# Gates and output projection of a hybrid decoder block rewritten as seven-block products in fp16 parts

## The chip, the cores and the metric

The kernel runs on one core of a Trainium2 chip. Its metric is the device time of one execution in microseconds, from three runs; beside it stands one execution taken by the hardware profiler. The engines are TensorE (matmuls; PE in rows), VectorE (DVE), ScalarE (ACT), GpSimd (POOL) and SyncE (SP, which issues the transfers). Each works through its own instructions in a fixed order.

## The reference, cut to what matters

One layer, 2048 positions of 1024 channels, float32:

```python
h = rmsnorm(x, norm_mix_g)
(lru_x, lru_gate, m_qk, m_v, m_o, m_i, m_f,
 s_q, s_k, s_v, g_a, g_b, g_c) = split(h @ w_in)          # g_*: 1024 columns each
ya = (rg_lru(conv(lru_x)) * gelu(lru_gate)) @ w_out_lru       # 256 -> 1024
yb = (sigmoid(m_o) * mlstm(conv(m_qk), m_v, ...)) @ w_out_mlstm
yc = stick_breaking_attention(s_q, s_k, s_v) @ w_out_sb
merged = sigmoid(g_a) * ya + sigmoid(g_b) * yb + sigmoid(g_c) * yc
x = x + merged @ w_o
hf = rmsnorm(x, norm_ffn_g)
gate, up = split(hf @ w_ffn_in)                            # 2 x 2816 columns
x = x + (silu(gate) * up) @ w_ffn_out
out = rmsnorm(x, final_norm_g)
```

## The kernel before

Channels lie on the 128 partitions, positions on the free axis, in four chunks of 512 (`CH`). Three stages follow one another.

**S** goes chunk by chunk: projections of h (`psd`), the mLSTM (`m`), the linear recurrence (`L`, `l`), attention of the chunk before (`a`, `attn`), the norm of the next chunk (`t`), and queries, keys and values (`S`); `ORD` is that order. Attention works in pieces of one head and one chunk of keys: per piece four score tiles (`pz`, two matmuls each), two sigmoids on ScalarE (`ka`, `be`), a scan on VectorE (`cb`), the product `be` x `cb` in turn on VectorE and GpSimd, transposes on TensorE (`pt`), a split into two parts (`ah` on ScalarE, `al` on VectorE) and eight matmuls into `pav`. Attention of the last chunk stands behind S in the code.

**G** and **G_out** go chunk by chunk too. Operands are float32 split into a high and a low part of type float32r; `dense` (L189) issues three matmuls per term, high by high, high by low, low by high. `weights` (L168, L176) loads each weight tile again for each chunk and splits it. A gate tile (`pg`, 24 matmuls) goes through a sigmoid and is multiplied by its branch projection (`py`, 6 matmuls); `po` is the output projection.

**F**, the feed-forward part, works on pairs of chunks. Two 2 x 2 block matrices are multiplied with seven block products instead of eight (`STEPS`, `blocks`), each product three fp16 matmuls per term (`product`, L864 to L866). `wforms` loads four weight blocks, forms their sums on GpSimd (`sm`), finds a power-of-two scale (a sum of squares, a one-column matmul `pse`, small integer steps `sce`, `scx`, `scf`) and writes seven blocks in two fp16 parts (`wh` on ScalarE, `wl` on VectorE). `F_input` does the same for the activations (`xq`, `tt`, `f`). F1 writes its results in such parts to DRAM (`fs` to `dA`); F2 reads them (`f<-dA`) once the scales of all of them are known.

A tile framework keeps dependences and buffers and sets each engine's order from the order of the code. PSUM has eight buffers of 128 x 512: two `d`, one `m`, two `z`, two `s`, one `av`. In G, `py` uses `m` for the first two chunks and `z` for the others, `pg` uses `d`.

## Time and profile before

| what | us |
|---|---|
| median of 3 runs (3026.48 to 3029.7) | 3026.51 |
| the profiled execution | 3026.73 |
| its span, first to last instruction | 3025.0 |
| TensorE busy in the span | 2838.8 |
| VectorE busy | 1962.6 |
| ScalarE busy | 1318.9 |
| GpSimd busy | 728.1 |

The span is shorter than the execution's time by 1.7 us. An engine is busy while an instruction with work runs on it; time in which it waits for a buffer or an input is not counted. The mean granted clock of TensorE was 0.963 of full speed.

### The profile page before, as it was taken

To read this page: it belongs to the slowest core of one execution; us is meant where nothing else is said; L and a number is where in the kernel's file an instruction comes from. 1 tells how busy PE (TensorE), PEld (TensorE's weight loads), DVE (VectorE), ACT (ScalarE), POOL (GpSimd) and SP (SyncE) were. 2 spreads that over 40 slices of the span, in tenths; PEclk is the share of its full clock that TensorE was granted. 3 is DMA by queue.
4 is the path that set the end of the run, shared out by engine and by line. 5 is a ranking of instruction groups with operands and counts; after the bars stand their busy time and mean duration, and the time that the engine had idled before them with its cause. 6 is when DMAs were issued, how large, how long until landed. Compare 5 with 4: busy or idle time off the path is not lost.

```text
span 3025.0 us, 36457 instructions
## 1 busy us (share of the span) xinstructions
PE 2838.8 (94%) x13405; PEld 1870.1 (62%) x13405; DVE 1962.6 (65%) x2793; ACT 1318.9 (44%) x1975; POOL 728.1 (24%) x876
## 2 busy tenths in 40 slices
PE   8999999999999999999998479999999996899996
PEld 7777878777877887888887134444444442344443
DVE  7677888987777765345343875555555554657667
ACT  4445464644554543223222444444444452434432
POOL 0022323322232210000000653233233231323221
PEclk9999999999999999999999699999999998899998
DMA  5454545354355325335324211222222226336433
GB/s 174 149 175 144 185 139 166 118 168 169 108 169 171 105 91 188 115 97 194 100 94 169 78 66 66 77 77 84 77 84 85 79 77 250 143 146 257 181 116 143
DMA packets 153171, 398.85 MB, mean 132 GB/s; under 512 B 18176, under 2 KB 38656, under 8 KB 144800
## 3 DMA queue, kind: packets, MB, share of 16 engines
q1 hardware_dynamic: 152992, 396.53, 38.0%
q8 instruction: 105, 1.72, 0.2%
q14 instruction: 74, 0.61, 0.1%
HBM read 307.79 MB, written 88.67 MB: 131 GB/s over the span
## 4 chain that ended last, share of the span: by engine, by line
PE 81%; DVE 8%; DMA 5%; issue 3%; ACT 2%; POOL 1%; SPq 0%; DVEq 0%; ACTq 0%; POOLq 0%
PE pfp L864 7%; PE pfp L866 7%; PE pfp L865 7%; PE pg L197 6%; PE pg L195 6%; PE pg L196 6%; PE pfq L864 3%; PE pfq L866 3%; PE pfq L865 3%; PE psd L195 3%; PE psd L197 3%; PE psd L196 3%; PE pt L689 2%; PE pfr L864 2%; PE pfr L865 2%
## 5 line engine op out<-in xcount | busy, mean ns | idle before, releaser
L176 DVE TENSOR_TENSOR wl<-wraw,wh 128x768 fp32r<-128x768 f32 (+2 forms) x232 | 285.1, 1230 | 282.7 <-ACT wh L168 281.9
L168 ACT ACTIVATE wh<-wraw 128x768 fp32r<-128x768 f32 (+2 forms) x232 | 238.6, 1030 | 462.0 <-PE pg L196 202.3
L864 PE MATMUL pfp<-f,wh 128*128 128x512 f16 x1056 | 403.4, 383 | 35.7 <-ACT f L908 22.4
L865 PE MATMUL pfp<-f,wh 128*128 128x512 f16 x1056 | 404.1, 383 | 8.3 <-DVE f L909 8.3
L866 PE MATMUL pfp<-f,wl 128*128 128x512 f16 x1056 | 401.0, 383 | 0.0
L864 PEld LDWEIGHTS <-wh 128*128 128x128 f16 x1848 | 182.3, 99 | 266.4 <-issue 34.3
L866 PEld LDWEIGHTS <-wl 128*128 128x128 f16 x1848 | 181.8, 98 | 235.7 <-issue 15.7
L865 PEld LDWEIGHTS <-wh 128*128 128x128 f16 x1848 | 182.1, 99 | 231.6 <-issue 24.1
L197 PE MATMUL pg<-hh,wl 128*128 128x512 f32 x768 | 305.5, 398 | 2.8 <-DVE wl L176 2.8
L195 PE MATMUL pg<-hh,wh 128*128 128x512 f32 x768 | 305.8, 399 | 1.2 <-ACT sgg L725 0.7
L196 PE MATMUL pg<-hl,wh 128*128 128x512 f32 x768 | 303.1, 395 | 1.6 <-POOL hl L176 1.6
L864 PE MATMUL pfq<-f,wh 128*128 128x512 f16 x528 | 201.7, 382 | 13.2 <-ACT wh L811 9.4
L866 PE MATMUL pfq<-f,wl 128*128 128x512 f16 x528 | 200.9, 382 | 4.1 <-DVE wl L812 4.1
L865 PE MATMUL pfq<-f,wh 128*128 128x512 f16 x528 | 201.9, 382 | 0.6 <-DVE f L909 0.6
L195 PE MATMUL psd<-hh,wh 128*128 128x512 f32 x448 | 183.9, 411 | 2.8 <-DVE scl L315 2.8
L826 POOL TENSOR_TENSOR sm<-raw 128x512 f32<-128x512 f32 (+1 forms) x46 | 66.1, 1436 | 496.8 <-DVE wl L812 380.1
L197 PE MATMUL psd<-hh,wl 128*128 128x512 f32 x448 | 180.8, 403 | 0.5 <-DVE wl L176 0.5
L196 PE MATMUL psd<-hl,wh 128*128 128x512 f32 x448 | 180.0, 402 | 0.0
L811 ACT ACTIVATE wh<-raw,scf 128x512 f16<-128x512 f32 (+1 forms) x154 | 116.1, 771 | 126.1 <-PE pfp L865 52.4
L197 PEld LDWEIGHTS pg<-hh,wl 128*128 128x128 f32 x768 | 145.8, 190 | 39.2 <-DVE wl L176 5.2
L196 PEld LDWEIGHTS pg<-hl,wh 128*128 128x128 f32 x768 | 144.7, 188 | 35.8 <-POOL hl L176 2.0
L195 PEld LDWEIGHTS pg<-hh,wh 128*128 128x128 f32 x768 | 144.6, 188 | 33.2 <-ACT sgg L725 0.9
(301 smaller groups left out, 6105.2 us busy)
## 6 DMA issues: line engine op xcount, KB each, us to landing
wraw<-in_wG SPq DMA_DIRECT2D x96, 512.0 KB, 3.5
f<-dA SPq DMA_DIRECT2D x22, 1792.0 KB, 14.5
wraw<-in_wS SPq DMA_DIRECT2D x56, 512.0 KB, 3.6
x<-in_xT SPq DMA_DIRECT2D x88, 256.0 KB, 4.0
raw<-in_wF SPq DMA_DIRECT2D x22, 1024.0 KB, 4.8
dA<-fs SPq DMA_DIRECT2D x44, 512.0 KB, 2.6
dA<-fs SPq DMA_DIRECT2D x22, 768.0 KB, 3.4
wraw<-in_wO SPq DMA_DIRECT2D x32, 512.0 KB, 5.3
```

Source lines behind the costliest of these rows:

```text
L168: nc.scalar.activation(dst, src, AF.Copy)
L176: (self.nc.gpsimd if pool else self.nc.vector).tensor_tensor(lo, src, hi.bitcast(F32), op=ALU.subtract)
L195: nc.tensor.matmul(ps, wh, hh, start=start and i == 0, stop=False)
L196: nc.tensor.matmul(ps, wh, hl, start=False, stop=False)
L197: nc.tensor.matmul(ps, wl, hh, start=False, stop=stop and i == n - 1)
L689: PE.transpose(pt[:, i * P : (i + 1) * P], As[i][:, js], self.idn)
L811: self.nc.scalar.activation(hi, x, AF.Copy, scale=s)
L826: G.tensor_tensor(sm[:, 0], a21, a22, op=ALU.add)
L864: mm(ps, wh[:, i, ks], f[:, j, 0], start=start and k == 0, stop=False, skip_group_check=True)
L865: mm(ps, wh[:, i, ks], f[:, j, 1], start=False, stop=False, skip_group_check=True)
L866: mm(ps, wl[:, i, ks], f[:, j, 0], start=False, stop=k == n - 1, skip_group_check=True)
```

## The change

Gates, branch projections and output projection are done like F: on pairs of chunks, seven block products, three fp16 matmuls per term. In the two pairs `gates` goes through 12 weight items (channel quarter i by branch), each 7 blocks of 12 matmuls and, four times 6 matmuls, the branch projection of the item before (`mix`, tile `py`). `project` has 6 items. `wforms` becomes a generator: `advance` steps it between block products, two items ahead, and steps other queues of work (`fill`) at a set rate: the attention of chunks 2 and 3 (0.45) beside the gates of the first pair, the inputs of the next product (0.9, 1.3), the parts of F1's results (0.8). Branch outputs y are stored once in float32 (`put_y`), and `y_parts` splits them per pair. The merged quad goes to DRAM in fp16 parts (`dM`) and is loaded as `mf`. The gates' inputs of the first pair, `H(0)`, are formed behind S. Scales of F2 and of the projection are per group (`scales`). In phase "G", `s` of PSUM has one buffer, for attention's `pt`; `pfq` takes the other (`q`), and `py`, `pse` and `pfr` take `m`.

```diff
+OSTEPS = [(0, 0, 3), (1, 0, 3), (0, 3, 1), (1, 3, 1), (2, 0, 4), (3, 0, 4)]
...
-    ORD = ["mLlatS"] * 4
+    ORD = ["mLltS", "mLlatS", "mLlatS", "mLlS"]
     PT = 6
-    NP = dict(d=2, m=1, z=2, s=2, av=1)
-    GT = "mzds"
+    NP = dict(d=2, m=1, z=2, s=1, q=1, av=1)
...
+    def psum(self, tag, name):
+
+        if tag == "s" and self.phase != "G":
+            tag = "sq"[self.flip]
+            self.flip ^= 1
+        return self.ps.tile([P, CH], F32, tag=tag, name=name, bufs=self.NP[tag])
...
-    def put_y(self, pool, i, c, y):
-        th = pool.tile([P, CH], FR, tag="yh", name="yh", bufs=1)
-        tl = pool.tile([P, CH], FR, tag="yl", name="yl", bufs=1)
-        self.split(th, tl, y, "A")
-        cs = slice(c * CH, (c + 1) * CH)
-        self.nc.sync.dma_start(self.dY[i, 0, :, cs], th.bitcast(F32))
-        self.nc.sync.dma_start(self.dY[i, 1, :, cs], tl.bitcast(F32))
+    def put_y(self, i, c, y):
+        self.nc.sync.dma_start(self.dY[i, :, c * CH : (c + 1) * CH], y)
...
                         As.append(at)
+                    yield
                     for j in range(NB):
...
+    def wforms(self, src, n, off, more=None):
...
+        yield
+        if more and self.gx:
+            mraw = more_load()
+        acc = self.cp.tile([P, 1], BF, tag="wacc", name="wacc", bufs=2)
...
+        yield
+        f = self.power(self.exponent(acc), off() if callable(off) else off)
+        m = f.shape[-1] - 1
+        w = ((wh, wl), f[:, m : m + 1])
+        yield
         if m == 1:
...
+    def next_weights(self):
+        k = self.at
+        w = self.work.pop(k).finish()
+        self.at = k + 1
+        self.load_item(k + 2)
+        if k + 1 in self.work:
+            self.work[k + 1].step()
+        return w
+
...
+    def advance(self):
+        if self.at in self.work:
+            self.work[self.at].step()
+        for f in list(self.fills):
+            f[2] += f[1]
+            while f[2] >= 1.0:
+                f[2] -= 1.0
+                f[0].step()
+            if f[0].done:
+                self.fills.remove(f)
...
+    PSG = dict(p="d", q="q", r="m")
...
+    def seven(self, q, t, put):
+
+        G = self.nc.gpsimd
+        b12, b11, b21, b22 = [q[:, i] for i in range(4)]
+        G.tensor_tensor(t, b12, b11, op=ALU.subtract)
+        put(B11, b11)
+        yield
+        put(T1, t)
+        G.tensor_tensor(t, b22, t, op=ALU.subtract)
+        yield
...
+            for (u, j), at in self.PLACE.items():
+                x = q[:, at]
+                V.scalar_tensor_tensor(x, x, gs[:, k + 4 * j : k + 4 * j + 1], R[u], op0=ALU.mult, op1=ALU.mult)
+            q0, kk = q, k
+            k = kk + 1
+            if k < KT // 2:
+                q = load()
+            yield
+            f = slot()
+            out.append(f)
+            yield from self.seven(q0, tt(), lambda i, x: self.split2(f[:, i, 0], f[:, i, 1], x))
+
...
+            for u in (1, 0):
+                y = self.gx.tile([P, 2, 2, CH], F16, tag="yt", name="ys", bufs=3)
+                self.split2(y[:, :, 0], y[:, :, 1], q[:, 2 * u : 2 * u + 2], s)
+                nc.sync.dma_start(self.dYs[cp, br, u], y)
...
+        def mix(n, br, ys, wm, inv, sg, aq):
+            u, j = [(1, 0), (1, 1), (0, 0), (0, 1)][n]
+            ps = self.psum("m", "py")
+            for k in range(2):
+                c = slice(k * 256 + j * P, k * 256 + j * P + P)
+                y = ys[u]
+                mm = nc.tensor.matmul
+                mm(ps, wm[:, 0, c], y[:, k, 0], start=k == 0, stop=False)
+                mm(ps, wm[:, 0, c], y[:, k, 1], start=False, stop=False)
+                mm(ps, wm[:, 1, c], y[:, k, 0], start=False, stop=k == 1)
+            a, s = aq[:, self.PLACE[u, j]], sg[u, j]
+            V.scalar_tensor_tensor(a if br == 0 else s, ps, inv, s, op0=ALU.mult, op1=ALU.mult)
+            if br:
+                G.tensor_tensor(a, a, s, op=ALU.add)
+
...
+                def then(step, ps, inv=inv, sg=sg, c=c):
+                    if step < 3:
+                        c[step] = gx.tile([P, CH], F32, tag="cm", name="cm", bufs=6)
+                        A.activation(c[step], ps, AF.Copy)
+                        return
+                    if step < 6:
+                        t = c[step - 3]
+                        V.tensor_tensor(t, ps, t, op=ALU.add)
+                        A.activation(t, t, AF.Sigmoid, scale=inv)
+                    else:
+                        t = gx.tile([P, CH], F32, tag="cm", name="cg", bufs=6)
+                        A.activation(t, ps, AF.Sigmoid, scale=inv)
+                    sg[self.DONE[step]] = t
+
+                prev = (br, ys, wm, invm, sg, aq)
+                order = [0, 1, 2, 5, 4, 3, 6]
+                if last:
+                    at = [partial(mix, n, *last) for n in range(4)]
+                    order = [0, at[0], 1, at[1], 2, at[2], 5, at[3], 4, 3, 6]
+                self.blocks([(w, hs, then)], KT // 2, [(o, 0) if isinstance(o, int) else o for o in order])
+                ys[0] = y_load(br, 0)
+            else:
+                for n in range(4):
+                    mix(n, *last)
+                    self.advance()
+            if last and last[0] == 2:
+                p = b // 3 - 1
+                todo.append(self.fill(self.forms(last[-1], tpm[:, p : p + 1], self.dM[cp, p], gx, 1, 2)))
...
+    def merged(self, cp, p, pool, tag, bufs):
+        f = pool.tile([P, 7, 2, CH], F16, tag=tag, name="mf", bufs=bufs)
+        self.nc.sync.dma_start(f, self.dM[cp, p])
+        return f
...
+        for q, p0, n in OSTEPS:
+            w, inv = self.next_weights()
+            if q not in xs:
+                x_load(q)
+            self.blocks([(w, fs[p0 : p0 + n], partial(then, q=q, inv=inv, last=p0 + n == KT // 2))], n)
...
+        def forms(i, cp, drain=False):
+            w = self.fill(self.forms(quads[cp], self.tp[cp][:, i : i + 1], self.dA[cp, i], fc, 2, 2), 0.8)
+            if drain:
+                self.drain(w)
+
+        for cp in range(2):
+            for b in range(4):
+                self.blocks([side(cp, b % 2, *self.next_weights())], 4)
+                if b % 2:
+                    forms(b // 2, cp)
+            if cp == 0:
+                self.drain()
+                self.phase = "F"
...
+        for _ in H(0, hs, hq, "d", hq):
+            pass
...
+        self.load_item(0)
+        self.load_item(1)
+        self.y_parts(0)
+        self.NBE = 6
+        with pool("ap2") as self.ap:
+            self.fill(self.attns(), 0.45)
+            forms = self.gates(0, hs)
+            self.drain()
+        xf = [[], []]
+        ge = se.enter_context(pool("ge", "right"))
+        for k in range(2):
+            if k:
+                self.y_parts(1)
+                forms = self.gates(1, hs)
+                self.drain()
+            mer = [self.merged(k, p, ge, "e", 3) for p in range(3)]
+            sg.close()
...
+            if k == 0:
+                hs = []
+                self.fill(H(1, hs, self.gz, "z", self.wk), 0.9)
+            else:
+                R = [self.spread(self.gz, self.rs2[u], "u", 2, "z") for u in range(2)]
+                self.fill(self.inputs(
+                    lambda u, i: self.dX1[u, i], self.gs2, R, xf[0], lambda: self.slot(0),
+                    lambda: self.wk.tile([P, 4, CH], F32, tag="qd", name="hq", bufs=2),
+                    lambda: self.gz.tile([P, CH], F32, tag="tt", name="ht", bufs=1),
+                ), 0.9)
+            self.project(k, mer)
+            self.drain()
+            sp.close()
```

Three places where the order of instructions changes. The first is VectorE ahead of the first gate. Before, these are the rows that end with the first gate's product with its branch projection, `m<-sgg,py` (`h`, `hl`: the next chunk's input; `al`, `cb`: attention):

```order
L247 SCALAR_TENSOR_TENSOR h_10317<-x,g_mix,R 128x512
L247 SCALAR_TENSOR_TENSOR h_10325<-x,g_mix,R 128x512
L176 TENSOR_TENSOR wl<-wraw,wh 128x1024
L176 TENSOR_TENSOR wl<-wraw,wh 128x768
L176 TENSOR_TENSOR hl<-h_10317,hh 128x512
L247 SCALAR_TENSOR_TENSOR h_10333<-x,g_mix,R 128x512
L247 SCALAR_TENSOR_TENSOR h_10341<-x,g_mix,R 128x512
L176 TENSOR_TENSOR al<-pt,ah 128x512 x3
L727 TENSOR_TENSOR m<-sgg,py 128x512
L176 TENSOR_TENSOR al<-pt,ah 128x512
L729 TENSOR_TENSOR sgg<-sgg,py 128x512
```

After, these end with the first add of a gate product, `cm<-pfr` (`ys`: parts of y; `wl`, `wm`: low parts of the weights):

```order
L788 SCALAR_TENSOR_TENSOR ys<-yq,ascf,ys 128x2x512
L788 SCALAR_TENSOR_TENSOR wl<-raw,scf,wh 128x1024
L788 SCALAR_TENSOR_TENSOR wl<-sm,scf,wh 128x1024
L788 SCALAR_TENSOR_TENSOR wl<-raw,scf,wh 128x512 x2
L788 SCALAR_TENSOR_TENSOR wl<-sm,scf,wh 128x512
L693 SCALAR_TENSOR_TENSOR cb<-ka,ones 128x513
L788 SCALAR_TENSOR_TENSOR wm<-mraw,mscf,wm 128x512
L693 SCALAR_TENSOR_TENSOR cb<-ka,cr,ones 128x513
L788 SCALAR_TENSOR_TENSOR wl<-raw,scf,wh 128x1024
L788 SCALAR_TENSOR_TENSOR wl<-raw,scf,wh 128x512
L701 TENSOR_TENSOR be<-be,cb 128x512
L1087 TENSOR_TENSOR cm<-pfr,cm 128x512
```

The inputs `hq` stand further ahead of these rows. What moved is that the parts of y, of the weights and of the gates' inputs now all precede the first gate.

The second place is TensorE where attention of the last chunk is worked on. Before, in the gates of the first chunks:

```order
L196 MATMUL pg<-hl,wh 128x512
L695 MATMUL pav<-ah,vt 128x512
L197 MATMUL pg<-hh,wl 128x512
L195 MATMUL pg<-hh,wh 128x512
L196 MATMUL pg<-hl,wh 128x512
L197 MATMUL pg<-hh,wl 128x512
L195 MATMUL py<-yh,wh 128x512
L659 MATMUL pz<-kt,qh 128x512
L660 MATMUL pz<-kt,ql 128x512
```

After, first at the end of the gates of the first pair, then where the projection of that pair begins (`pfp<-mf`):

```order
L1064 LDWEIGHTS wm
L1064 MATMUL py<-yt,wm 128x512
L715 MATMUL pav<-ah,vt 128x512
L716 MATMUL pav<-al,vt 128x512
L709 MATMUL pt<-idn,be 128x128 x4
L678 MATMUL pz<-kt,qh 128x128
L679 MATMUL pz<-kt,ql 128x128
L678 MATMUL pz<-kt,qh 128x256
```

```order
L716 MATMUL pav<-al,vt 128x512
L709 MATMUL pt<-idn,be 128x128 x4
L715 MATMUL pav<-ah,vt 128x512
L716 MATMUL pav<-al,vt 128x512
L709 MATMUL pt<-idn,be 128x128 x4
L715 MATMUL pav<-ah,vt 128x512
L716 MATMUL pav<-al,vt 128x512
L895 LDWEIGHTS wh
L895 MATMUL pfp<-mf,wh 128x512
```

Matmuls of attention stood among those of `pg` and `py`. Now 54 pairs of `pav` stand between the last `py` and the first `pfp<-mf`, with no product of the gates or the projection among them.

The third place is TensorE in the gates of the second pair, at an item's branch projection and at the next scale (LDWEIGHTS loads the stationary operand):

```order
L1063 MATMUL py<-yt,wm 128x512
L1064 LDWEIGHTS wm
L1064 MATMUL py<-yt,wm 128x512
L895 LDWEIGHTS wh
L895 MATMUL pfp<-f,wh 128x512
L896 LDWEIGHTS wh
L896 MATMUL pfp<-f,wh 128x512
```

```order
L897 LDWEIGHTS wl
L897 MATMUL pfp<-f,wl 128x512
L767 LDWEIGHTS ones_383
L767 MATMUL pse<-wacc,ones_383 128x1
L895 LDWEIGHTS wh
L895 MATMUL pfq<-f,wh 128x512
```

Between the two pieces lies one block of 12 matmuls, `pfp`. `py` and the `pse` after it use the one buffer `m`. Before, 24 matmuls `pg` lay between two `py`:

```order
L195 MATMUL pg<-hh,wh 128x512
L196 MATMUL pg<-hl,wh 128x512
L197 MATMUL pg<-hh,wl 128x512
L195 MATMUL py<-yh,wh 128x512
L196 MATMUL py<-yl,wh 128x512
```

## Rows read from the trace of the kernel before

**Rows 1.** The page: span, busy time by engine, TensorE's share in fortieths of the span.
```profile
span 3025.0 us, 36457 instructions
...
PE 2838.8 (94%) x13405; PEld 1870.1 (62%) x13405; DVE 1962.6 (65%) x2793; ACT 1318.9 (44%) x1975; POOL 728.1 (24%) x876
...
PE   8999999999999999999998479999999996899996
```

**Rows 2.** By stretch: window, length, busy PE, PEld, DVE, ACT, POOL, clock, DMA.
```profile
0.00:653.00 653.00, 618.89 (x3293) 511.35 (x3294) 525.97 (x856) 337.92 (x563) 158.41 (x292) 0.95 0.48 155
...
653.00:1126.00 473.00, 461.17 (x2186) 375.18 (x2186) 359.69 (x440) 244.03 (x433) 123.21 (x259) 0.99 0.43 141
...
1250.00:1600.00 350.00, 349.69 (x1515) 283.75 (x1514) 147.29 (x180) 104.44 (x139) 5.64 (x4) 1.00 0.35 117
...
1650.00:1824.00 174.00, 108.00 (x412) 46.26 (x411) 137.40 (x139) 69.64 (x78) 90.68 (x55) 0.76 0.22 76
...
1824.00:2544.00 720.00, 719.22 (x3365) 326.29 (x3364) 416.37 (x568) 336.84 (x426) 226.62 (x155) 1.00 0.22 83
...
2544.00:2600.00 56.00, 16.58 (x73) 7.08 (x71) 18.46 (x41) 16.96 (x21) 11.03 (x8) 0.66 0.71 287
...
2985.00:3025.00 40.00, 18.43 (x82) 11.67 (x80) 27.21 (x48) 9.26 (x15) 0.00 (x0) 0.73 0.28 105
```

**Rows 3.** The same view for the instructions of tile pav.
```profile
0.00:653.00 653.00, 40.59 (x124) 21.88 (x124) 6.14 (x9) 5.36 (x9) 0.95 0.48 155
...
653.00:1126.00 473.00, 64.21 (x196) 36.04 (x196) 4.77 (x7) 4.18 (x7) 0.99 0.43 141
```

**Rows 4.** The same view for the instructions of tile pt, one stretch.
```profile
653.00:1126.00 473.00, 54.82 (x348) 42.77 (x348) 59.01 (x98) 50.63 (x96) 0.99 0.43 141
```

**Rows 5.** VectorE's instructions by form: count, busy us and mean ns, idle before.
```profile
L674 DVE TENSOR_TENSOR_SCAN cb<-ka,cr,ones 128x513 f32<-128x513 f32 x96 | 125.0, 1312 | 10.6 <-ACT ka L664 8.7 <-issue 1.8
...
L812 DVE SCALAR_TENSOR_TENSOR wl<-raw,scf,wh 128x512 f16<-128x512 f32 x132 | 103.6, 793 | 4.2 <-ACT wh L811 4.2
...
L176 DVE TENSOR_TENSOR al<-pt,ah 128x512 fp32r<-128x512 f32 x112 | 74.3, 682 | 47.9 <-ACT ah L168 47.6
...
L812 DVE SCALAR_TENSOR_TENSOR fs<-aq,ascf,fs 128x1024 f16<-128x1024 f32 x44 | 59.2, 1346 | 78.9 <-ACT fs L811 78.9
...
L812 DVE SCALAR_TENSOR_TENSOR wl<-sm,scf,wh 128x384 f16<-128x384 f32 x88 | 53.4, 611 | 0.0
...
L682 DVE TENSOR_TENSOR be<-be,cb 128x512 f32<-128x512 f32 x48 | 41.3, 860 | 3.4 <-DVE cb L674 0.9 <-ACT be L665 0.5
...
L904 DVE SCALAR_TENSOR_TENSOR xq<-xq,gs,Rf 128x512 f32<-128x512 f32 x32 | 39.4, 1282 | 4.0 <-DMA xq<-dX 3.9
...
L929 DVE SCALAR_TENSOR_TENSOR aq<-pfp,scf,aq 128x512 f32<-128x512 f32 x44 | 32.8, 746 | 42.0 <-PE pfp L866 42.0
...
L812 DVE SCALAR_TENSOR_TENSOR wl<-raw,scf,wh 128x1024 f16<-128x1024 f32 x22 | 31.2, 1418 | 10.3 <-ACT wh L811 10.3
...
L909 DVE TENSOR_TENSOR f<-tt,f 128x1536 f16<-128x1536 f32 x8 | 15.7, 1959 | 2.1 <-ACT f L908 2.1
...
L807 DVE TENSOR_SCALAR scf<-scx 128x2 int32<-128x2 int32 x22 | 10.0, 453 | 0.4
```

**Rows 6.** DMA issues of the page: count, KB each, us to landing.
```profile
f<-dA SPq DMA_DIRECT2D x22, 1792.0 KB, 14.5
```

**Rows 7.** TensorE's waits, 1640 to 1824: total us, times, longest.
```profile
PE pfp L864 <- ACT f L908: 22.4, 5, 8.9
```

**Rows 8.** TensorE's waits, 2540 to 2600.
```profile
PE pse L795 <- ACT fs L789: 36.1, 1, 36.1
```

**Rows 9.** The chain that ended last, 2540 to 2600: start, us, what.
```profile
2543.15 14.67 DMA dA<-fs
...
2560.40 11.47 DMA dA<-fs
```

**Rows 10.** GpSimd's instructions by form.
```profile
L827 POOL TENSOR_TENSOR sm<-sm,raw 128x512 f32<-128x512 f32 x38 | 62.4, 1643 | 3.0
```

More of the change, by code (lines that the diff above doesn't have):

```diff
@@ L71, in setup @@
         self.dX2 = dr.tile([KT, 2, P, CH], F32, name="dX2")
+        self.rs1 = [cp.tile([P, NB], F32, name=f"rs1{c}") for c in range(NCH)]
+        self.rs2 = [cp.tile([P, NB], F32, name=f"rs2{c}") for c in range(NCH)]
+        nc.scalar.activation(self.rs1[0], self.nhalf, AF.Square)
     def first_constants(self):
@@ new lines, in inputs, with load @@
+    def inputs(self, src, gs, R, out, slot, quad, tt):
+        V = self.nc.vector
+        def load():
+            q = quad()
+            for (u, j), at in self.PLACE.items():
+                self.nc.sync.dma_start(q[:, at], src(u, k + 4 * j))
+            return q
+        k = 0
+        q = load()
+        yield
+        for k in range(KT // 2):
+            for (u, j), at in self.PLACE.items():
+                x = q[:, at]
[3 more added lines that the diff above has]
+            if k < KT // 2:
+                q = load()
+            yield
+            f = slot()
+            out.append(f)
+            yield from self.seven(q0, tt(), lambda i, x: self.split2(f[:, i, 0], f[:, i, 1], x))
@@ new lines, in forms, with put @@
+    def forms(self, aq, t_out, dram, pool, nt, nf):
+        nc, V = self.nc, self.nc.vector
+        acc = self.cp.tile([P, 1], BF, tag="aacc", name="aacc", bufs=2)
+        j = pool.tile([P, 2, CH], F16, tag="fs", name="fj", bufs=nf)
+        self.squares(aq.rearrange("p i n -> p (i n)"), acc, j.rearrange("p e n -> p (e n)").bitcast(mybir.dt.uint8))
+        yield
+        yield
+        t = self.exponent(acc, "a")
+        V.tensor_copy(t_out, t)
+        s = self.power(t, self.off, "a")[:, 0:1]
+        yield
+        def put(i, x):
+            f = pool.tile([P, 2, CH], F16, tag="fs", name="fs", bufs=nf)
+            self.split2(f[:, 0], f[:, 1], x, s)
+            nc.sync.dma_start(dram[:, i], f)
+        yield from self.seven(aq, pool.tile([P, CH], F32, tag="tt", name="tt", bufs=nt), put)
@@ new lines, in at @@
+        def at():
+            R = self.stat(0, xs)
+            rs = self.rs1[0]
+            self.constants()
+            self.mix_constants()
+            return R, rs
+        for c in range(NCH):
+            st = self.S(c, hs, at if c == 0 else None)
+            for step in self.ORD[c]:
+                if step == "m":
+                    self.mlstm(c, st)
+                elif step == "L":
+                    st["lru"]()
+                elif step == "l":
+                    self.lru(c, st)
+                elif step == "S":
+                    st["sb"]()
+                elif step == "a":
+                    for _ in self.attn(c - 1):
+                        pass
+                elif step == "t" and c < NCH - 1:
+                    self.stat(c + 1)
+            if c < NCH - 1:
+                hs = self.h_of_chunk(c + 1)
@@ new lines, in run, with H @@
+        sh.close()
+        self.fa = self.ctx.enter_context(pool("fa", "right"))
+        hq = sx.enter_context(pool("hq", "right"))
+        def H(k, out, p, tag, quad):
+            R = [self.spread(p, self.rs1[2 * k + u], "u", 2, tag) for u in range(2)]
+            return self.inputs(
+                lambda u, i: self.I["xT"][2 * k + u, i], self.gs1, R, out, lambda: self.slot(0),
+                lambda: quad.tile([P, 4, CH], F32, tag="qd", name="hq", bufs=2),
+                lambda: p.tile([P, CH], F32, tag="tt", name="ht", bufs=1),
+            )
@@ new lines, in run @@
+        hs = []
+        for _ in H(0, hs, hq, "d", hq):
+            pass
+        sx.close()
+        sm.close()
+        sa.close()
+        self.wk = self.ctx.enter_context(pool("wk", "right"))
+        self.phase = "G"
+        self.tpm = [cp.tile([P, KT // 2], I32, name=f"tpm{k}", bufs=1) for k in range(2)]
+        self.tp = [cp.tile([P, NPAIR], I32, name=f"tp{k}", bufs=1) for k in range(2)]
+        self.items, self.work, self.at, self.fills = self.weight_items(), {}, 0, []
+        sg, se, sp = [ExitStack() for _ in range(3)]
@@ new lines, in run @@
+        se.close()
+        self.fl = self.ctx.enter_context(pool("fl"))
+        with pool("fc") as self.fc:
+            R = [self.spread(self.fc, self.rs2[2 + u], "tt", 2, "z") for u in range(2)]
+            self.fill(self.inputs(
+                lambda u, i: self.dX1[2 + u, i], self.gs2, R, xf[1], lambda: self.slot(1),
+                lambda: self.fc.tile([P, 4, CH], F32, tag="q1", name="hq", bufs=1),
+                lambda: self.fc.tile([P, CH], F32, tag="tt", name="ht", bufs=2),
+            ), 1.3)
+            self.F1(xf)
@@ L1151, in tile_trunk, with __init__, step, finish @@
+        with pool("fd") as self.fc:
+            for k in range(2):
+                self.F2(k)
+class Work:
+    def __init__(self, gen):
+        self.gen, self.done, self.value = gen, False, None
+    def step(self):
+        if not self.done:
+            try:
+                next(self.gen)
+            except StopIteration as e:
+                self.done, self.value = True, e.value
+    def finish(self):
+        while not self.done:
+            self.step()
+        return self.value
 def tile_trunk(tc, ins, out):
@@ L1190, in _layout @@
     a["wPe"] = piece(*FGROUPS[-1])
+    a["wO"] = piece(0, KT // 2, wm)
     def col(v):
```

576 lines of the change are left out of this document (286 added, 290 removed).

## The prediction

> **What bounds the kernel now.** The page's head comes first: TensorE is busy for 94% of the span, VectorE for 65%, and the fortieths show TensorE full nearly everywhere [rows 1]. So I asked for the stretches where it isn't, and what the full ones are made of. The table by stage [rows 2] gives it. The mixers (0 to 653 us) hold TensorE for 619 us. Gates and output projection (653 to about 1654) run it at 97 to 100%. The way into the feed-forward part (1650 to 1824) has 108 us of matmuls at a granted clock of 0.76 in 174 us. F1 (1824 to 2544) is full. The passage to F2 (2544 to 2600) has 17 busy us in 56, the end 18 in 40.
>
> Two paces follow from the full stretches [rows 2]. In 1250 to 1600, nothing but gates and projection in f32r, 1515 matmuls take 349.69 us: 0.231 us each. In 1824 to 2544, feed-forward products in fp16, 3365 take 719.22 us: 0.214 us. So TensorE bounds three quarters of the span, and a change here is worth (matmuls saved) less (TensorE time newly left empty).
>
> The Trainium skill ("TensorE: Matmul & The Clock Gate", section "Back-to-back issue gap") gives the warm isolated gap of a 512-column matmul as N/2.4 + 2.5 ns, about 216 ns, with no term for the type; by that estimate the two kinds run alike and only the smaller count counts, about 83 us by it. The trace agrees for fp16 and not for f32r, so the measured pair of paces is used.
>
> **The gain in matmuls.** Gates, branch projections and output projection go from 2304 + 576 + 768 = 3648 matmuls at 0.231 (842 us) to 2016 + 576 + 672 = 3264 at 0.214 (698 us): 144 us off, if the new ones are fed as densely. The rest of the account is whether they are. I go stage by stage and give each a low, a taken and a high value.
>
> **S, the mixers.** Attention's 40 pieces (one head, one key chunk) issue eight matmuls into pav each. The window to 653 has 124 of them, 15.5 pieces, the next 196, the rest [rows 3]. After, 12 pieces are left in S. A piece's TensorE time: in 653 to 1126 the trace has 2186 matmuls in 461 us [rows 2], 348 of them transposes [rows 4]. The other 1838 at 0.231 take 425, so a transpose gets about 0.11, and a piece of 16 wide matmuls (pz as many as pav) and 14 transposes 5.3 us. 3.5 pieces less take 18 us from 653. The splits of y that leave are VectorE work of 0.68 us beside a full TensorE: nothing. Low 625, **636**, high 660.
>
> **T1, from the last projection of S to the first gate product.** This is new: the gates' inputs are formed in series, where before the next chunk's h was ready. On VectorE: 16 scalings that now read their factor from PSUM, 0.75 as aq<-pfp, against 1.28 as xq with both inputs in SBUF (12 us); 28 low parts of 512 columns at about 0.70, between a third of f<-tt and aq<-pfp (20); six low parts of y at 1.35 (8); low parts of one and a half weight items (8); three attention pieces that the order puts here (some 24, of 9.7 for a full one, below); small integer steps (6) [rows 5]. That is 78 us, beside 16 us of TensorE. Nothing else covers it. Loads and hand-overs at the ends add some: low 80, **92**, high 115.
>
> **Gates of the first pair.** An item is 84 products and 24 of the branch projection: 108 x 0.214 = 23.1 us; twelve take 277, and 11.5 pieces of attention beside them 61: 338. VectorE has per item three adds like al's 0.68 (2.1), four reads of py (3.0), weight parts (5.2 + 0.8), a third of the merged quad's low parts (1.6) and small integer steps at up to 0.45 (2.5): 15 of 23 us, plus 9.7 per piece [rows 5] (four scans 5.25, two of four multiplications 1.7, four al 2.7). Together 293 of 338: close, so some waits show. Low 345, **365**, high 405: 27 us of waits over its sum.
>
> **The tail of attention.** The order has 108 of the 224 pav matmuls behind the last py and ahead of the first projection: 13.5 pieces with no products between. Before, the same pieces stood among gate matmuls and cost only their 5.3 us. Here VectorE sets the pace: 13.5 x 9.7 = 131 us [rows 5], while TensorE has 72. Low 125, **138**, high 190. This is the largest loss.
>
> **Projection, twice.** 336 matmuls, 72 us. VectorE beside them: 42 updates of x at 0.75 (31), weight parts of 16 column blocks at 0.79 + 0.61 (22), the inputs of the next stage, four times 4 x 0.75 + 7 x 0.70 (32), small steps (10): 95 us [rows 5]. So VectorE bounds it: low 85, **92 and 94**, high 115. The SP queue has the parts of the last merged quad ahead of the load of 1792 KB that feeds the projection; such a load landed after 14.5 us [rows 6]. In the first pair that hides behind the tail; in the second some of it shows.
>
> **Gates of the second pair.** 277 us of TensorE, VectorE 182: no bound in sums. But py, the exponents' pse and the accumulator pfr now share the one PSUM buffer "m", seven uses per item. Before, py came again after 24 gate matmuls, 5.5 us later; now a block of 12 lies between, 2.6 us, and VectorE may have weight parts of 1.42 us ahead of the read, two at a time [rows 5]. No row has this spacing. Bounds: nothing, as in the full stretches; or one such instruction per use, 7 x 0.7 on average, 5 us per item. I take 2.3, nearer to nothing because most uses find VectorE a third empty: low 283, **305**, high 340.
>
> **F.** Before, 1654 to 3025 is 1371 us. Lost in it: in 1650 to 1824, 174 less 412 x 0.214 = 86; in the passage 56 less 73 x 0.214 = 40; at the end 40 less 82 x 0.214 = 22 [rows 2]. The entry's loss is waits for f [rows 7] and the lower clock behind them; its inputs now come beside the projection, so I leave 10 of it, with the first products single-sided and VectorE nearly as loaded as TensorE. In the passage TensorE waits 36.1 us for an activation [rows 8], and the chain shows why: stores of fs that take 14.67 and 11.47 us behind loads [rows 9]. Scales are now per group, but the f loads still precede the last stores in SP's queue: I leave 30. The weights loaded again go beside a full TensorE. 1371 - 76 - 10, less 7 of projection and statistics that still lie behind 1654: low 1258, **1278**, high 1302.
>
> **The sum.** 636 + 92 + 365 + 138 + 92 + 305 + 94 + 1278 = 3000. The profiled execution took 3026.73 us against a span of 3025.0 and a median of 3026.5, so 2 us lie around the span: **3002 us**, 0.8% faster. As an account: 144 in matmuls, 93 in F, and 29 of waits and statistics that lay between 653 and 1654 (1001 less 842 less 24.5 pieces of 5.3) are gained; lost are 92 - 16 = 76 in T1, 138 - 72 = 66 in the tail, 42 in the projections, 55 in waits of the gates. The rest, 2, is S against its moved pieces.
>
> **The rivals.**
> *Waits hide.* Stretches run at their work: T1 82, gates 348 and 288, tail 131, projections 88 twice, S 630, F 1260: **2917**. For it: F1's full 720 us under VectorE at 58%. Against: the gates have VectorE at 87% in the first pair.
> *The single buffer "m" (slower).* If each item waits 5.6 us and not 2.3, 24 items cost 80 us more: **3082**. It decides at 1 us more per item (24 items against the 24 us forecast), less than one weight part. For it: the spacing of 2.6 us and an in-order VectorE; against: the small work of the other uses.
> *The tail runs slower than VectorE's sum.* With TensorE waiting at each piece the clock may fall as in 1650 to 1824 (0.76) [rows 2]; at 1.2 GHz its 72 us are 144, and with a single "s" buffer some of it adds: tail 190 to 200, **3057**. GpSimd works more as well (sums of 1.64 each [rows 10]), and VectorE was slow beside it: xq 1.28 with two SBUF inputs [rows 5].
> The Trainium skill ("SBUF — State Buffer", section "Who interferes with whom") says that VectorE and GpSimd share a port pair under an exclusive lock. By that rule the added GpSimd sums would block VectorE's two-input forms; xq against aq<-pfp agrees in direction.
> *It cancels.* Losses of 18 to 31 us more than taken, spread thin: 3020 to 3033.
>
> **Chances.** A measurement tells 0.2%, 6 us, from no change. Forecast (2945 to 3020, its own range) 0.45; waits hide 0.12; cancels 0.08; buffer "m" 0.21; tail 0.14. So faster 0.57, same 0.08, slower 0.35. The range takes in both sides' cases with the bounds of T1, tail and "m": 2900 to 3105.
>
> **What would show it.** TensorE's rows after: fp16 gates at 0.214 per matmul; an empty stretch of about 75 us behind S; some 140 us with only pz, pt and pav, VectorE over 90% busy; projections with VectorE ahead of TensorE in the waits; py or pse waiting for VectorE's reads in the gates; the first F products at a granted clock near 1. Wrong would be: gates over 330 us in the second pair, a tail beyond 190, or T1 under 50.

## The result and the profile after

The changed kernel takes 3325.7 us against 3027.1 us (medians of four runs each): a ratio of 1.098, interval 1.097 to 1.100. The forecast was 3002 us. The profiled execution has a span of 3326.9 us and a mean granted clock of 0.908, against 0.963.

First the table by stretch of the changed kernel, the counterpart of [rows 2] (window, length, busy PE, PEld, DVE, ACT, POOL, clock, DMA). The cuts lie where the tiles change: gates from 728, the last `py` at 1126, `pfp<-mf` from 1352, gates of the second pair from 1474, F from 1926.

```profile
0.00:621.00 621.00, 590.44 (x3140) 486.13 (x3141) 468.74 (x796) 296.92 (x485) 126.35 (x245) 0.95 0.45 144
621.00:728.00 107.00, 51.90 (x157) 30.91 (x155) 76.01 (x121) 56.29 (x92) 47.52 (x69) 0.54 0.49 155
728.00:1126.00 398.00, 362.35 (x1670) 180.30 (x1670) 281.74 (x390) 225.17 (x380) 195.47 (x226) 0.96 0.34 110
1126.00:1352.00 226.00, 150.34 (x418) 90.48 (x417) 146.76 (x201) 102.20 (x189) 77.97 (x152) 0.58 0.22 71
1352.00:1442.00 90.00, 80.00 (x341) 33.98 (x341) 63.79 (x100) 36.30 (x62) 37.70 (x33) 0.94 0.55 202
1442.00:1474.00 32.00, 9.30 (x44) 6.08 (x43) 8.41 (x22) 15.48 (x19) 11.88 (x10) 0.64 0.49 157
1474.00:1790.00 316.00, 287.29 (x1292) 124.50 (x1292) 168.12 (x270) 154.86 (x229) 112.90 (x87) 0.98 0.38 127
...
2260.00:2850.00 590.00, 533.22 (x2418) 237.80 (x2416) 309.42 (x480) 260.63 (x369) 150.81 (x112) 0.95 0.22 80
2850.00:2890.00 40.00, 12.29 (x51) 5.19 (x49) 20.30 (x36) 15.07 (x23) 10.80 (x8) 0.66 0.73 290
```

Set against the forecast's sum, stage by stage, in us:

| stage | forecast | measured | difference |
|---|---|---|---|
| S | 636 | 621 | -15 |
| T1, S to the first gate | 92 | 107 | +15 |
| gates, first pair | 365 | 397 | +32 |
| tail of attention, to the projection | 138 | 226 | +88 |
| projection, first pair | 92 | 90 | -2 |
| between the pairs | no term | 32 | +32 |
| gates, second pair (to the last py, 1799) | 305 | 325 | +20 |
| last merged quad and projection, second pair | 94 | 127 | +33 |
| F | 1278 | 1401 | +123 |

Two stages hold 211 of the 326 us, and the larger one is F, whose products the change hardly touches. The row 2260 to 2850 shows it: before, F1 ran with TensorE busy 719 of 720 us; now 533 of 590. TensorE's waits of 2100 to 2850 name the reason (total us, times, longest):

```profile
PE pfp L895 <- DVE aq L1166: 58.0, 14, 8.4
PE pfp L895 <- ACT cm L1171: 4.8, 7, 0.7
```

So the first product of an item waits for VectorE to empty its PSUM buffer (`aq`). What VectorE and ScalarE do just then is in ScalarE's timeline of one such wait, 2305.0 to 2313.7 for TensorE (start, us, instruction, idle before and what ended it):

```profile
2301.22 0.72 ACT L787 ACTIVATE fs<-aq,ascf 128x512 f16<-128x512 f32 x1 [0.96 <-DMA dA<-fs]
2303.15 0.72 ACT L787 ACTIVATE fs<-aq,ascf 128x512 f16<-128x512 f32 x1 [1.21 <-DMA dA<-fs]
2305.07 0.72 ACT L787 ACTIVATE fs<-tt,ascf 128x512 f16<-128x512 f32 x1 [1.19 <-DMA dA<-fs]
2306.78 0.72 ACT L787 ACTIVATE fs<-tt,ascf 128x512 f16<-128x512 f32 x1 [0.99 <-DMA dA<-fs]
2308.68 0.72 ACT L787 ACTIVATE fs<-aq,ascf 128x512 f16<-128x512 f32 x1 [1.18 <-DMA dA<-fs]
2310.22 1.95 ACT L1165 ACTIVATE aq<-cm,scf 128x512 f32<-128x512 f32 x3 [0.82 <-DVE fs L788]
```

Each part of F1's result waits until a store has freed one of two `fs` buffers, 1.9 us a part. The sigmoids that write the next `aq` stand behind the parts in ScalarE's order, and the quad that they write is read by those parts.

The other stage is the tail. Two views of it: waits of TensorE in 1126 to 1352, then of ScalarE in 1126 to 1340 (the last TensorE row is the wait for the load that feeds the projection).

```profile
PE pav L716 <- DVE al L191: 25.5, 21, 4.4
PE pav L715 <- ACT ah L183: 23.7, 32, 3.7
PE pfp L895 <- DMA mf<-dM: 11.8, 1, 11.8
```

```profile
ACT ah L183 <- PE pt L709: 60.4, 37, 3.6
```

VectorE is busy 147 us in 226, not far above the 131 of the forecast, and some 23 us of the 147 are not attention: 12 of the 16 scalings `hq` of the second pair's inputs, with their low parts. The work goes round: TensorE waits for `ah` and `al`, ScalarE for the next `pt`, at a granted clock of 0.58, at which TensorE's own part takes 150 us. 54 key blocks, four to a piece, in 213 us are 3.9 us each.

### The profile page after: what moved, and what is told of

The parts are those of the page before. It is cut to its first block, busy times and chain, and to the rows that moved or that the text cites. A ratio compares the mean times of both kernels' runs of the same rounds, so it can differ in the third digit from the quotient of the medians.

```text
span 3326.9 us, 37305 instructions
## 1 busy us (share of the span) xinstructions
PE 2877.9 (87%) x13132; PEld 1557.0 (47%) x13132; DVE 2170.7 (65%) x3400; ACT 1554.3 (47%) x2437; POOL 1088.9 (33%) x1183
## 5 line engine op out<-in xcount | busy, mean ns | idle before, releaser
L895 PE MATMUL pfp<-f,wh 128*128 128x512 f16 x1440 | 559.6, 389 | 96.3 <-DVE aq L1166 58.0
L896 PE MATMUL pfp<-f,wh 128*128 128x512 f16 x1440 | 559.1, 388 | 3.1 <-DVE f L785 3.1
L897 PE MATMUL pfp<-f,wl 128*128 128x512 f16 x1440 | 553.9, 387 | 4.6 <-DVE wl L788 4.4
L896 PEld LDWEIGHTS <-wh 128*128 128x128 f16 x2744 | 272.1, 99 | 465.2 <-issue 173.7
L895 PEld LDWEIGHTS <-wh 128*128 128x128 f16 x2744 | 272.6, 100 | 357.4 <-issue 30.9
L787 ACT ACTIVATE wh<-raw,scf 128x512 f16<-128x512 f32 (+3 forms) x278 | 210.1, 778 | 163.1 <-DVE scf L779 148.3
L788 DVE SCALAR_TENSOR_TENSOR wl<-raw,scf,wh 128x512 f16<-128x512 f32 (+3 forms) x278 | 250.5, 915 | 50.3 <-ACT wh L787 49.6
L895 PE MATMUL pfq<-f,wh 128*128 128x512 f16 x720 | 273.1, 379 | 4.9 <-DVE xf L1232 2.2
L896 PE MATMUL pfq<-f,wh 128*128 128x512 f16 x720 | 273.1, 379 | 0.2 <-DVE f L785 0.2
L760 ACT ACTIVATE wl<-raw 128x2048 uint8<-128x2048 f32 (+2 forms) x86 | 153.8, 1788 | 165.4 <-issue 105.6
L788 DVE SCALAR_TENSOR_TENSOR wl<-sm,scf,wh 128x384 f16<-128x384 f32 (+2 forms) x224 | 188.8, 846 | 0.0
L787 ACT ACTIVATE wh<-sm,scf 128x384 f16<-128x384 f32 (+2 forms) x224 | 164.7, 740 | 6.8 <-POOL sm L816 5.3
L895 PE MATMUL pfr<-f,wh 128*128 128x512 f16 x360 | 138.6, 385 | 7.5 <-DVE sce L769 7.2
## 6 DMA issues: line engine op xcount, KB each, us to landing
f<-dA SPq DMA_DIRECT2D x22, 1792.0 KB, 11.3
```

The costliest lines, as they stand in the source:

```text
L760: self.nc.scalar.activation(junk, src, AF.Square, accum_out=acc)
L787: self.nc.scalar.activation(hi, x, AF.Copy, scale=s)
L788: self.nc.vector.scalar_tensor_tensor(lo, x, s, hi, op0=ALU.mult, op1=ALU.subtract)
L895: mm(ps, wh[:, i, ks], f[:, j, 0], start=start and k == 0, stop=False, skip_group_check=True)
L896: mm(ps, wh[:, i, ks], f[:, j, 1], start=False, stop=False, skip_group_check=True)
L897: mm(ps, wl[:, i, ks], f[:, j, 0], start=False, stop=k == n - 1, skip_group_check=True)
```

## The experiments

Each version was run once, beside a run of the kernel before on the same chip, except the last, which was run four times. Differences are against 3326 us. The kernel before took 3020 to 3026 us in these runs, by chip, and 3027 us beside the changed kernel, so a difference of up to 7 us between two chips tells nothing. They go in three groups, then sums, then one piece of the change alone.

**F1's parts.** `fs6` gives them six buffers in F1's steady part; the pool is changed after the first two items to make room:

```diff
-            w = self.fill(self.forms(quads[cp], ..., fc, 2, 2), 0.8)
+            w = self.fill(self.forms(quads[cp], ..., self.fc, self.NTT, self.NFS), 0.8)
...
+        self.drain()
+        self.next_fc()          # NFS = 6 from here
         for b in range(4, 2 * NPAIR - 2):
```

> Six buffers in place of two for the parts of F1's results (fs) from F1's third item on; the first two items keep two, and what is still queued is finished before the change of pool. Theory A (the two buffers: each part goes ScalarE 0.72, VectorE 0.75, store 2.0 us, and with two of them a part takes 1.95 us, ahead of the aq that TensorE waits for): the burst of some eight parts before each gate item goes from about 16 to 7 us, the waits of pfp for aq (58 us in all) go below 10, F1 gets 60 to 85 us shorter, 3240 to 3266 us. Theory B (the parts are stepped too late, at 0.8 per block, whatever the buffers): at most 20 us, 3306 us or more.

3252.5 us, 73 less. The waits for `aq` fell from 58.0 to 1.1 us; one wait of 13.6 us is new, at the change of pool. The buffers are a cause. `rate16` only doubles the rate:

```diff
-            w = self.fill(self.forms(...), 0.8)
+            w = self.fill(self.forms(...), 1.6)
```

> F1's parts are stepped at 1.6 per block in place of 0.8, still two buffers. Theory A (two buffers): 14 parts of 1.95 us are a chain of 27 us and the first write of the next quad comes after about 18 us, so waits of pfp for aq stay, 0 to 25 us gained, 3300 to 3326 us. Theory B (stepped too late): the waits go, 60 to 85 us gained, 3240 to 3266 us.

3321.6 us: no gain, the waits for `aq` are 55.3 us. Stepping faster alone does not help. `fsnow` keeps two buffers and finishes each pair's parts before the next code:

```diff
             w = self.fill(self.forms(...), 0.8)
-            if drain:
-                self.drain(w)
+            self.drain(w)
```

> F1's parts are put out at once behind their blocks, as the code before did, in seven stores with two buffers. Theory A (two buffers): like rate16, 0 to 25 us gained, with the chain of parts now ahead of weight parts too, so perhaps a loss up to 20. Theory B (stepped too late): 60 to 85 us gained.

3241.1 us, 85 less, a miss for theory A as stated: two buffers are enough if the parts come early and one pair after the other. In 590 us of F1 TensorE now does 2763 matmuls and is full, at 0.2135 us each; in the same window fs6, with its one wait of 13.6 us, does 2642 and the changed kernel 2412:

```profile
2100.00:2690.00 590.00, 590.00 (x2763) 267.79 (x2762) 359.22 (x540) 294.42 (x416) 175.93 (x132) 1.00 0.22 78
```

That left the question why 1.6 per block fails and all at once does not. Both queues are stepped in turn, so the parts of the two pairs alternate through the two buffers, and the first pair's last part, which its next `aq` needs first, comes at the end of the whole chain. `chain16` tests this:

```diff
-            for cp in range(2 * up):
-                forms(i, cp)
+            if up:
+                self.fill(both(i, dict(quads)), 1.6)   # parts of pair 0, then of pair 1
```

> F1's parts from its third item on: those of the second pair are stepped only when those of the first are out, at 1.6 per block, with two buffers; rate16 stepped both pairs in turn at 1.6. Theory A (the parts of both pairs alternate through two buffers, so that the first pair's last part comes at the end of a chain of 27 us and not of 14): the waits of pfp for aq go below 15 us, 55 to 85 us gained, 3240 to 3270 us. Rival (stepping is late in itself, and only putting them out at once helps): like rate16, 0 to 15 us gained.

3267.2 us, 59 less, against 4 of rate16; the waits for `aq` are 12.2 us, not 55.3. So the loss is two buffers together with two queues that take turns in them: more buffers, or no turns, recover most of it. fsnow takes away the stepping and the turns at once, so what stepping costs without turns is seen only in chain16: at most the 26 us by which it is behind fsnow, and chain16 leaves the first two items as they were.

**The tail.** `ord3` takes chunk 2's attention back into S:

```diff
-    ORD = ["mLltS", "mLlatS", "mLlatS", "mLlS"]
+    ORD = ["mLltS", "mLlatS", "mLlatS", "mLlaS"]
...
-        for c in (2, 3):
+        for c in (3,):
```

> Attention of chunk 2 (12 pieces) goes back into S, beside the mixers of chunk 3; only chunk 3's 16 pieces are left beside the gates. The order then has 20 pav matmuls behind the last branch projection in place of 108. Theory A (attention alone is bound by hand-overs and a lower clock, beside products it costs its matmuls): the tail goes from 226 to about 45 us, S grows by 12 x 5.3 = 64 to 85 us, in all 90 to 130 us gained, 3196 to 3236 us. Rival (attention costs its hand-overs wherever it stands, since S is full of waits too): S grows by 150 us or more, 30 us gained or less.

3227.0 us, 99 less. The first gate product starts at 801 us, not 728: 12 pieces cost S 72 us, 6.0 each, close to the 5.3 of matmuls. The tail fell from 226 to 58 us. A piece in the tail cost 16, with the second pair's inputs among the pieces; a piece beside products cost 6.

`s2` lets `pt` alternate between two PSUM buffers and leaves `pz` one:

```diff
-    NP = dict(d=2, m=1, z=2, s=1, q=1, av=1)
+    NP = dict(d=2, m=1, z=1, y=1, s=1, q=1, av=1)
...
+        elif name == "pt":
+            tag = "sy"[self.flip]
+            self.flip ^= 1
```

> In the gates' phase attention's transposes pt get two PSUM buffers and its scores pz one (before: one and two). The order then has 80 pav matmuls behind the last branch projection, not 108. Theory A (the one buffer of pt: pt, ah, al and the next pt hand it round in turn): a piece in the tail falls from 15.8 us (213 us for 13.5) to 10 or 11, near VectorE's 9.7; the tail from 226 to 115 to 125 us, 3215 to 3235 us in all. Rival (the lower clock and the order set the pace, not the buffer): ten pieces at 15.8, tail about 170, 3265 to 3280 us.

3243.1 us, 83 less: the tail went to 146 us, with ten pieces in it at 13.6 us. That lies between the two theories. Three and a half pieces got out of the tail and the rest got 14% faster. TensorE's waits for `al` in it are 9.1 us and for `ah` 3.3, not 25.5 and 23.7, so the one buffer was a cause, but VectorE's 9.7 isn't reached. The granted clock rose with it, from 0.58 to 0.69:

```profile
1122.00:1268.00 146.00, 92.95 (x313) 61.35 (x312) 110.90 (x153) 74.22 (x139) 48.28 (x108) 0.69 0.28 92
```

`arate` steps attention twice as often:

```diff
-            self.fill(self.attns(), 0.45)
+            self.fill(self.attns(), 0.9)
```

> Attention beside the first gates is stepped at 0.9 per block in place of 0.45. Theory A (its pace is set by the hand-overs through pt's one buffer, not by how often it is stepped): the order still has 96 pav matmuls behind the last branch projection (108 before), 12 pieces of 16 us; 0 to 30 us gained, 3296 to 3326 us. Rival (the rate left the tail behind): the tail halves, 100 us gained.

3310.6 us, 15 less, of which 7 may be the chip (the kernel before took 3019.8 us on it). The rate didn't leave the tail behind; 96 pav are still there.

**Between the pairs.** TensorE waits 18.0 us in one piece there, for the sum of squares of y. `yearly` moves that work ahead of the projection:

```diff
-                self.y_parts(1)
                 forms = self.gates(1, hs)
...
             mer = [self.merged(k, p, ge, "e", 3) for p in range(3)]
+            if k == 0:
+                self.y_parts(1)
```

> The parts of y for the second pair are formed ahead of the first projection, not behind it. Theory A (the 32 us between the first projection and the next gates are these parts, which nothing covers): the stretch falls below 12 us and the tail or the projection grows by 5 or less, 15 to 25 us gained. Rival (the work only moves: the projection waits for them instead): no gain, 3320 us or more.

3337.4 us, 11 more: the rival. The stretch from the projection to the gates fell to 11 us, but the projection grew from 90 to 123 (the row starts 8 us ahead of it):

```profile
1344.00:1476.00 132.00, 92.87 (x365) 38.02 (x365) 95.91 (x166) 56.07 (x93) 55.69 (x47) 0.82 0.52 185
```

What moved is not the parts of y alone. These are the scalings `hq` of the second pair's inputs, first in the tail of the changed kernel (1126 to 1352), then in the projection of yearly (1344 to 1476), and TensorE's waits for VectorE's updates of x in the projection of each:

```profile
L972 DVE SCALAR_TENSOR_TENSOR hq<-hq,gs,psr 128x512 f32<-128x512 f32 x12 | 8.3, 743 | 1.7 <-DMA hq<-in_xT 1.3 <-PE psr L257 0.5
...
L972 DVE SCALAR_TENSOR_TENSOR hq<-hq,gs,psr 128x512 f32<-128x512 f32 x16 | 11.1, 739 | 1.9 <-DMA hq<-in_xT 1.9
```

```profile
PE pfp L895 <- DVE xq L1128: 2.2, 5, 0.6
...
PE pfp L895 <- DVE xq L1128: 17.0, 7, 10.9
```

In yearly four of the six parts of y are formed in the tail and none of the second pair's inputs: all of those come beside the projection.

`lvy` leaves the work out altogether, and the second gates read the first pair's parts:

```diff
-            nc.sync.dma_start(y, self.dYs[cp, br, u])
+            nc.sync.dma_start(y, self.dYs[0, br, u])
...
-                self.y_parts(1)
                 forms = self.gates(1, hs)
```

> Leaves out the parts of y for the second pair: its gates read those of the first pair (loads, mixes and products stay). Yearly only moved this work. Theory A (formed in series between two stages, it costs the 32 us that stand between the first projection and the next gates): 22 to 32 us gained, 3294 to 3304 us. Rival (something else would hold the gates there, the weights of the first items or the loads): less than 10 us gained.

3307.4 us, 18 less, between the two.

**Sums.** `combo1` is ord3, fsnow and yearly together, with the edits shown.

> ord3, fsnow and yearly together. If the three losses are independent, 98 + 85 + 20 us come off: 3115 to 3130 us. If F1's loss or the tail only moves into the next stage, 3150 us or more. Faster than the kernel before is expected by no theory.

3163.6 us, in the range of the second branch. But 99 + 85 - 11 off would be 3153, so the gains at F1 and at the tail nearly add up; the first branch missed mainly because it counted yearly as a gain. `combo3` is ord3, fsnow and s2.

> ord3, fsnow and s2 together (without yearly); the order has no pav behind the last branch projection. If the tail's loss is gone for good: 3326 - 98 - 85 and some 40 more for what ord3 left of the tail and of waits beside the gates: 3090 to 3130 us. If attention with two buffers slows the products that it stands beside, 3140 us or more. The kernel before stays faster in either case, since the second pair, which has no attention beside it, took 484 us from the first projection's end to F against 421 us of full matmuls for two chunks before.

3152.0 us, outside the first expectation and in the range of the second, though the stages do not show its reason. No pav is left behind the last `py`, and the first pair's gates with attention and what follows (802 to 1217) take 415 us, where ord3's gates and tail (801 to 1257) took 456. The projection behind them takes 124 us and not 93: with no tail, all 16 scalings `hq` stand in it, where ord3 had 5. So s2 gives nothing once the tail is short: fsnow and ord3 alone would be 3142 if they add up, or 3153 by combo1 less yearly's 11; that pair was not run. Its stages carry the rest of the answer (T1, first projection, between the pairs, last quad):

```profile
694.00:802.00 108.00, 63.56 (x206) 40.07 (x205) 84.77 (x117) 63.26 (x111) 54.66 (x96) 0.64 0.39 127
...
1217.00:1341.00 124.00, 89.83 (x358) 38.48 (x358) 95.22 (x154) 53.75 (x92) 58.11 (x48) 0.84 0.56 198
1341.00:1373.00 32.00, 9.44 (x45) 6.16 (x43) 8.52 (x23) 15.78 (x20) 11.87 (x10) 0.63 0.50 158
...
1686.00:1731.00 45.00, 18.14 (x68) 8.68 (x67) 27.00 (x57) 16.68 (x25) 16.03 (x14) 0.74 0.37 136
```

`combo4` adds more buffers for the parts, six in F1's steady part and three, not two, in the second pair's merged quads:

```diff
-                todo.append(self.fill(self.forms(..., self.dM[cp, p], gx, 1, 2)))
+                todo.append(self.fill(self.forms(..., self.dM[cp, p], gx, 1, 3 if cp else 2)))
```

> combo3 with six buffers for F1's parts from the third item on (as fs6, but put out at once) and three, not two, for the merged quads' parts of the second pair. If the parts' chain through few buffers also holds up the second pair's projection (parts of the last quad from 1805 to 1822, TensorE empty for 19 of 26 us): 5 to 10 us off there, and 5 to 15 off the passage to F2: 10 to 25 us below combo3. Rival (what holds it up is the order, the spread for the next inputs behind the parts): no more than 5 us below combo3.

3150.3 us: the rival, 2 us. From the last `py` to F it takes 129 us, and combo3 124, so the third buffer gave nothing there. `lvcy` is combo3 without the second pair's parts of y, as in lvy.

> The same left out of combo3. Theory A: 20 to 30 us below its 3152, 3122 to 3132 us, still 100 above the kernel before, for the other losses (inputs behind S, waits in the gates, the last merged quad ahead of its projection) are in it as before. Rival: 3142 us or more.

3121.7 us, 30 less: the hand-over between the pairs is a loss of its own, and the version is still 97 us above the kernel before.

**One piece of the change alone.** F's entry was the part of the forecast's gain that doesn't need new gates. `bearly` is the kernel before with F's first inputs ahead of the last output projection:

```diff
                         self.fr = s0.enter_context(pool("fr", "right"))
+                        self.F_constants()
+                        xf = self.F_input(0, ...)
                     self.G_out(c, mer)
-                self.F_constants()
-                xf = self.F_input(0, ...)
```

> The kernel before, with one piece of the change alone: F's inputs of the first pair are formed ahead of the last chunk's output projection in the code, so that they run beside its matmuls (the order puts 16 of the 20 xq rows of that pair among xr<-po). Theory (the entry of F, 86 us lost of 174, is a loss that the rewrite of gates and projection is not needed for): 30 to 55 us gained, 2970 to 2997 us. Rival (VectorE, with 137 us of work between 1650 and 1824, stays the bound of the entry, so the loss only moves to the second pair's inputs): 15 us gained or less, 3010 us or more.

2996.0 us against 3027.1 us, ratio 0.991, interval 0.989 to 0.993: 1% less than the kernel before, with all four runs (2991 to 3002) below its seven (3022 to 3033), and at the upper edge of the expectation. In the first 150 us behind 1650 TensorE now works 119 us at a clock of 0.87, where [rows 2] had 108 in 174 at 0.76:

```profile
1650.00:1800.00 150.00, 118.78 (x492) 56.22 (x493) 110.90 (x120) 69.88 (x84) 77.28 (x49) 0.87 0.27 97
```

## Why the prediction was wrong, point by point

- **Gain in matmuls: right.** The fp16 products of the gates run at the feed-forward pace: in 1474 to 1790 nineteen of twenty start 0.216 us after the one before. S was 15 us better than taken, below its low of 625. (A slip that the sum does not hang on: before, gates and projection ran TensorE at 94 to 100%, not at 97 to 100.)
- **F: the step that failed most.** The forecast took 1371 us of before and subtracted what it knew. It counted the matmuls and checked the entry, but put the parts of F1's results at nothing. They went from three stores through one large buffer to seven through two small ones, and from one place in the order to steps in turn between products. Before, these parts were in nobody's way: TensorE was full. fs6, fsnow and chain16 show that 59 to 85 of the 123 us are this. F's first items (1926 to 2100) are part of the rest: 685 matmuls take 146 us at full pace, so 28 are lost where the forecast left 10. I read that from the trace and tested nothing there. The passage, taken at 30, came as forecast: one wait of 25.3 us, behind stores of `fs`.
- **The tail: right place, wrong size.** "VectorE sets the pace" was the step that failed. It set 9.7 us a piece as the work; the measured 16 is a round through three engines with one PSUM buffer and a clock of 0.58. The rival "the tail runs slower than VectorE's sum" named both, and had them at 190 to 200, with 144 us of TensorE at the low clock where 150 were measured; a tail beyond 190 was also one of the forecast's signs of being wrong. s2 shows the buffer's share in the waits; the clock's own share was not separated. The load that the forecast hid behind the tail is 11.8 us at its end.
- **T1: VectorE's sum right, the length not.** VectorE's 78 us came as 76, but in 107 us and not 92. TensorE's longest waits are 11.3 us for a load of keys (`kt`) and 10.1 for `al`. No run tested it.
- **Gates of the first pair: sized too low.** 397 against 365. The forecast's own sum had VectorE at 87% and left 27 us for waits; it was 59 over 338: TensorE stood empty for 36 us and was busy for 24 more than the sum, at a clock of 0.96. VectorE was busy 282 us of 398. No run tested it.
- **Projection, first pair: the number right by luck.** The forecast put 95 us of VectorE beside it and took 92. In the changed kernel VectorE was busy 64 us there, because 12 of the 16 `hq` of the next inputs had been done in the long tail. Where all 16 stand in it, in combo3, VectorE is busy the 95 us of the forecast and the stage takes 124.
- **Between the pairs: a missing term.** T1 was priced for the first pair; the second pair's parts of y were not priced at all, 32 us. lvy and lvcy put their cost at 18 to 30; yearly shows that moving them into the tail only pushes the second pair's inputs out of it.
- **Projection, second pair: 127 for 94.** The load that was to show here does not: TensorE has no wait for `mf` from 1799 to 1926. It waits 12.8 us for the updates `xq`, and 9.0 for the spread of the next inputs (`psr` for `ndg`). Parts of the last merged quad go through two `fs` buffers here too; combo4's third buffer gave nothing, so the order (on VectorE the spread stands behind the parts, and the next inputs ahead of the updates) is left as the reading, not shown.
- **The buffer "m": not what made the second gates long.** In 1474 to 1800 TensorE waits 19 us for readers of this buffer, 1.6 per item where the forecast had 2.3 and the rival 5.6. All waits are 32 us; the stage took 325 and not 305 because TensorE was also busy 294 us there and not 277.
- **The clock** was lower in every stretch with long gaps: 0.54 in T1, 0.58 in the tail, 0.64 between the pairs. The forecast spoke of it for the tail and for F's entry. What it costs by itself no run separates.

The sign came out wrong because the losses were taken from a list of what the change adds, and the largest two were in what it re-times: F1's parts and attention. Three kinds of stretch were priced at VectorE's sum with little or nothing added, and each took far longer than VectorE was busy in it: 107 us for 76 in T1, 226 for 147 in the tail, 124 for 95 in combo3's projection.

What stays open: with the tail and F1's parts put right, some 130 us remain (combo3). The trace puts them into T1 (108 us, of which TensorE is busy 64 at a clock of 0.64), the first projection with the second pair's inputs (124), the hand-over (32), the last quad (45), and F's first items. Only the hand-over was tested, and the last quad's buffers, without gain.

## What to carry to other kernels

Work that is cut into pieces and put between products is not free because an engine has room on average: look at what each piece holds (a buffer, the next quad, a place in an in-order engine) until its store has landed, and whether the first consumer needs its last piece. A stretch with few products can take far longer than its busiest engine's sum: look for the round through engines and buffers that sets its pace. When a stretch shrinks, ask what other work had been done in it and where that goes now. And when a rewrite bundles a good idea with a large one, try the good idea alone.

## What the runs showed of the hardware that was not expected

VectorE's time for one form changes with what GpSimd does meanwhile where both inputs are in SBUF, and not where one is in PSUM. In 1926 to 2100, with GpSimd busy 98 of 174 us, the low parts `f<-hq` took 1143 ns and the scalings `hq`, which read one operand from PSUM, 737 (VectorE's groups of that stretch):

```profile
L785 DVE TENSOR_TENSOR f<-hq,f 128x512 f16<-128x512 f32 x16 | 18.1, 1143 | 0.1
...
L972 DVE SCALAR_TENSOR_TENSOR hq<-hq,gs,psr 128x512 f32<-128x512 f32 x16 | 11.4, 737 | 0.0
```

In the tail (1126 to 1340) `f<-hq` took 764 and `hq` 743. Taken one by one over the whole trace of the changed kernel, the 21 `f<-hq` during which no GpSimd instruction ran took 675 to 692 ns, and the 43 others 1066 on average, up to 1759. For `hq` the two means are 739 and 741, for the updates `xq<-pfp`, which also read PSUM, 745 and 744. So the forecast's 0.70 for such low parts holds alone, and a GpSimd instruction beside one can add over 1 us to it. This is the direction that the Trainium skill gives ("SBUF — State Buffer", section "Who interferes with whom": an exclusive port pair that VectorE shares with GpSimd). The trace agrees instruction by instruction; no run here took GpSimd's work away, so what it costs the whole kernel is not shown.
